# Bringing the inverted triangular blocks back with full transposes instead of small products

## The chip, the cores and the metric

The kernel runs on one of the eight cores of a Trainium2 chip. The metric is device time in microseconds (us) of one execution. A core has five engines with instruction queues of their own that work strictly in order: TensorE (PE; its weight loads are listed as PEld), VectorE (DVE), ScalarE (ACT), GpSimd (POOL) and SyncE (SP, which here only issues transfers).

## The reference, cut to what matters

One layer of a hybrid backbone runs on 640 tokens (128 of a prompt, 512 of a sample). Its second branch is a two-directional recurrence over the tokens, for 8 heads with 64 features:

```python
def step(S, inp):
    r_t, w_t, k_t, v_t, a_t, b_t = inp
    sa = jnp.einsum('bhvk,bhk->bhv', S, a_t)
    S = S * w_t[:, :, None, :] + sa[..., None] * b_t[:, :, None, :] + v_t[..., None] * k_t[:, :, None, :]
    return S, jnp.einsum('bhvk,bhk->bhv', S, r_t)
```

Each step needs `sa`, which depends on the state that the step before left. If 64 tokens are taken as one chunk, all `sa` of a chunk solve a linear system whose matrix is unit triangular, 64 by 64. There are 10 chunks, 8 heads and 2 directions, so 160 such matrices have to be inverted.

## The kernel before, in words

The heads are treated in four pairs, i = 0 to 3. For a pair, `rw_a` projects the inputs and `rw_b` prepares them. `rw_c` writes the within-chunk products of 40 matrices (2 heads, 2 directions, 10 chunks) to `MS`, 128 partitions by 40 by 128; its left upper 64 by 64 holds the triangular part. `rw_i` inverts the two diagonal 32 by 32 blocks of each, `rw_m` joins them to the inverse of the whole and runs the recurrence over the chunks, `rw_e` and `rw_f` give the outputs. `rw_d` transposes keys and values between them (L593, L603) and copies them out (L595, L604).

`rw_i` is the part that changes. It puts one block on each partition: 40 blocks of the first diagonal position (b = 0) on partitions 0 to 39, 40 of the second on 64 to 103. L620 does this with 64 small products by the identity, L622 copies the result to `X` as `X[block, s, t]`. Then come 30 elimination steps on DVE, each a product of two broadcast slices (L629) and an add into `X` (L632). All 60 instructions depend on the one before. Column t of the blocks is final after step t - 1, and from then on L638 brings it back: for each t and each b a product with `X[rows, :, t]` as the stationary operand and the identity as the moving one, 64 in all, each of 40 by 32. Three PSUM banks collect 11, 11 and 10 columns, and L640 copies each bank into `MS`, first DVE for b = 0, then ACT for b = 1.

Nothing fixes the order of the queues by hand. The program is written as a list, a scheduler estimates when each instruction could run, and gives every engine a fixed order. The recurrence is written with high priority. Between its pieces lie the *fills*, 24 blocks of the dense input projection (`values`, `qk_head`, `gate`), which keep PE at work: each is 48 products with 128 stationary columns (L202, L203, L204) on weights which SP loads (L183), ACT rounds (L186) and POOL splits (L187). At the end of a group DVE takes two columns out of PSUM first (L232), then ACT copies the rest.

Of the kernel before, what the change touches and what calls it, by code (L numbers as in the profile page):

```python
# [14 lines left out]
ALU = mybir.AluOpType  # L15
# [20 lines left out]
HJ, HR = 99, 6  # L36
# [30 lines left out]
def tile_layer(ctx, tc, x_prompt, x_sample, cache_k, cache_v, state_rwkv, c, c_ctx, w_ada, b_ada, w_in,  # L67
# [4 lines left out]
    nc = tc.nc  # L72
# [54 lines left out]
    def ada_steps(c0, n, load, ps, small):  # L127
        """n modulation columns from c0, a step for each block of the conditioning vector"""
# [62 lines left out]
    def dense(slabs, kb, xh, xl, evac, extra=0, new=None):  # L191
        """products of a block of weights; the operand's extra leading columns go with the first half"""
# [30 lines left out]
    # the shift of either conditioning in two columns, then the scaled tokens  # L223
# [3 lines left out]
    def project_in(w, evac, scale=1.0, new=None):  # L227
        """a block of the input projection: evac(columns of tokens, products, the shift's part times scale)"""
# [33 lines left out]
    with tc.tile_pool(name="start", bufs=1) as sp, tc.tile_pool(name="psS", bufs=2, space=PSUM) as psS:  # L262
# [21 lines left out]
        def ada1(ps, was, turned, dst, bias):  # L284
            """modulation of 256 features for each of was, the conditioning vector in two halves"""
# [28 lines left out]
        # silu of the conditioning vectors, as the stationary operand  # L314
# [7 lines left out]
        # the scaled input, and with it the first two blocks  # L322
# [27 lines left out]
        # the shift, and its part in the first blocks  # L350
# [21 lines left out]
        # derived per-feature scalars  # L372
# [51 lines left out]
    # the low-rank inputs: what rounds exactly twice over, for the two parts of the weights, and the rest  # L424
# [36 lines left out]
    def rsqrt_heads(x, op, floor):  # L461
        """1/sqrt of the sums of x over each head's features, token-major [token, block, head]"""
# [9 lines left out]
    def spread(rn):  # L472
        """token-major [token, block, head] to feature-major, every feature of a head alike"""
# [12 lines left out]
    def rw_b(i):  # L486
        r, kr, v, upw = (R[i][k] for k in ("r", "kr", "v", "upw"))
        # normalised key
# [65 lines left out]
        # bonus weights  # L554
# [8 lines left out]
    def rw_c(i):  # L563
        AR, BK, v, vrev = (R[i][k] for k in ("AR", "BK", "v", "vrev"))
        # within-chunk products
# [19 lines left out]
    def rw_d(i):  # L585
        BK, v, vrev = (R[i][k] for k in ("BK", "v", "vrev"))
        # token-major values and keys
# [20 lines left out]
    def rw_i(i):  # L608
        MS = R[i]["MS"]
        # inverse of the unit triangular part, in blocks of 32, a block on each partition  # L610
# [3 lines left out]
        prev = None  # L614
        for y in range(2):
# [5 lines left out]
            for b in range(2):  # L621
                (nc.scalar.copy if b else nc.vector.tensor_copy)(out=X[64 * b:64 * b + 40, :, 16 * y:16 * y + 16],  # L622
                                                                 in_=ps[64 * b:64 * b + 40].rearrange("p t s -> p s t"))
# [821 lines left out]
```

## Time and profile before

| | us |
|---|---|
| three runs | 1439.34, 1444.38, 1454.81 |
| median | 1444.38 |
| span of the profiled execution | 1442.3 |
| PE busy | 1334.4 (93%) |
| DVE busy | 928.1 (64%) |
| ACT busy | 535.7 (37%) |
| POOL busy | 556.6 (39%) |

The profiled execution is listed by its span, from the first to the last instruction; a time of its own is not listed beside it. The span lies 2.1 us under the median of the three runs. A page of the profile gives shares over the whole span. The four inversions lie between 127 and 613 us, so the answers that matter are those for stretches in this part, and the order of single instructions in them.

### The profile page before, as it was taken

How to read it: one execution, taken by the hardware profiler on the slowest of the kernel's cores; microseconds unless marked ns; L12 is line 12 of the kernel's file. 1: busy time of each engine (PE TensorE's matmuls, PEld its weight loads, DVE VectorE, ACT ScalarE, POOL GpSimd, SP SyncE). 2: the span in 40 equal slices, each digit the busy share in tenths (PEclk: the TensorE clock that was granted, in tenths of full speed). 3: DMA queues.
4: the chain of work that ended last, by engine and by line, in shares of the span. 5: the costliest groups of instructions: out<-in, count | busy, mean ns of one | idle time of the engine just before them, and what ended most of it. 6: DMA issues, size and time to landing. Idle time of an engine off the chain costs nothing.

```text
span 1442.3 us, 26589 instructions
## 1 busy us (share of the span) xinstructions
PE 1334.4 (93%) x10545; PEld 1139.9 (79%) x10545; DVE 928.1 (64%) x1719; ACT 535.7 (37%) x1126; POOL 556.6 (39%) x423
## 2 busy tenths in 40 slices
PE   6989998899998999999989998968999999999994
PEld 5877877777787778777978777748988989989983
DVE  2476856675568563743136744497897987778777
ACT  3442342234323431242345532254443433434432
POOL 3251225332443132111331036546654735536623
PEclk9997999899799995999999999978999999999997
DMA  9410212211122110111786767513232232322222
GB/s 304 128 56 23 60 38 76 81 55 38 30 82 90 33 47 21 55 51 51 223 268 198 250 205 254 190 45 117 74 103 70 78 95 64 91 67 80 67 68 86
DMA packets 157456, 144.58 MB, mean 100 GB/s; under 512 B 10490, under 2 KB 128020, under 8 KB 157332
## 3 DMA queue, kind: packets, MB, share of 16 engines
q1 hardware_dynamic: 147490, 127.85, 28.9%
q10 hardware_dynamic: 9842, 15.03, 3.1%
q8 instruction: 83, 1.36, 0.4%
q14 instruction: 41, 0.34, 0.1%
HBM read 121.06 MB, written 19.69 MB: 98 GB/s over the span
## 4 chain that ended last, share of the span: by engine, by line
PE 38%; DVE 13%; issue 5%; POOL 3%; DMA 2%; ACT 2%; SPq 1%; DVEq 0%; ACTq 0%; POOLq 0%
PE ps_d L1262 8%; PE ps_e L1262 3%; PE ps_d L202 2%; PE ps_d L203 2%; PE ps_d L204 2%; PE acc L1298 2%; DVE sums L1235 2%; PE acc L1296 2%; PE acc L1297 2%; PE acc L1098 2%; DVE zacc L1311 2%; PE S L964 1%; PE T L988 1%; PE ps_m L749 1%; POOL wl L210 1%
## 5 line engine op out<-in xcount | busy, mean ns | idle before, releaser
L187 POOL TENSOR_TENSOR wl<-ws,wh 128x512 fp32r<-128x512 f32 x100 | 138.6, 1387 | 435.6 <-ACT wh L186 374.8
L210 POOL TENSOR_TENSOR wl<-sums,wh 128x512 fp32r<-128x512 f32 x88 | 136.8, 1560 | 39.2 <-ACT wh L209 37.3
L1262 PE MATMUL ps_d<-oph,wh 128*128 128x320 f32 x440 | 138.5, 315 | 10.6 <-DVE u L1274 5.0
L210 POOL TENSOR_TENSOR wl<-wu,wh 128x512 fp32r<-128x512 f32 x63 | 88.6, 1406 | 142.8 <-ACT wh L209 129.4
L1262 PE MATMUL ps_d<-oph,wl 128*128 128x320 f32 x440 | 137.6, 313 | 0.6 <-POOL wl L210 0.6
L1262 PE MATMUL ps_d<-opl,wh 128*128 128x320 f32 x440 | 137.4, 312 | 0.7 <-DVE opl L210 0.7
L186 ACT CAST wh<-ws 128x512 fp32r<-128x512 f32 x100 | 61.8, 619 | 181.8 <-PE ps_d L203 89.5
L203 PE MATMUL ps_d<-hl,wh 128*128 128x322 f32 (+1 forms) x368 | 128.1, 348 | 0.0
L202 PE MATMUL ps_d<-hh,wh 128*128 128x322 f32 (+1 forms) x368 | 126.6, 344 | 0.7 <-ACT raw L395 0.7
L204 PE MATMUL ps_d<-hh,wl 128*128 128x322 f32 (+1 forms) x368 | 127.0, 345 | 0.0
L1262 PEld LDWEIGHTS ps_d<-oph,wh 128*128 128x128 f32 x440 | 83.7, 190 | 15.0 <-ACT wh L209 7.7
L1262 PEld LDWEIGHTS ps_d<-opl,wh 128*128 128x128 f32 x440 | 83.7, 190 | 2.0 <-POOL hf L1192 1.1
L1262 PEld LDWEIGHTS ps_d<-oph,wl 128*128 128x128 f32 x440 | 83.7, 190 | 1.4 <-POOL wl L210 1.2
L1296 PE MATMUL acc<-wh,gh 128*128 128x512 f32 x195 | 77.5, 398 | 2.5 <-ACT gh L209 2.5
L209 ACT CAST wh<-sums 128x512 fp32r<-128x512 f32 x88 | 54.6, 620 | 65.3 <-PE ps_e L1262 25.3
L202 PEld LDWEIGHTS ps_d<-hh,wh 128*128 128x128 f32 x368 | 74.6, 203 | 5.2 <-issue 1.5
L203 PEld LDWEIGHTS ps_d<-hl,wh 128*128 128x128 f32 x368 | 74.3, 202 | 4.5 <-issue 0.9
L204 PEld LDWEIGHTS ps_d<-hh,wl 128*128 128x128 f32 x368 | 74.0, 201 | 4.3 <-issue 0.8
L1297 PE MATMUL acc<-wl,gh 128*128 128x512 f32 x195 | 77.3, 397 | 0.0
L1298 PE MATMUL acc<-wh,gl 128*128 128x512 f32 x195 | 76.1, 397 | 0.5 <-DVE gl L210 0.5
L203 PE MATMUL ps_x<-hl,wh 128*128 128x322 f32 (+1 forms) x224 | 75.5, 337 | 0.0
L204 PE MATMUL ps_x<-hh,wl 128*128 128x322 f32 (+1 forms) x224 | 74.6, 334 | 0.5 <-POOL wl L187 0.5
(425 smaller groups left out, 3532.2 us busy)
## 6 DMA issues: line engine op xcount, KB each, us to landing
wu<-in_w_up_dram SPq DMA_DIRECT2D x42, 512.0 KB
ws<-in_w_in_dram SPq DMA_DIRECT2D x76, 256.0 KB
wa<-in_w_ada_dram SPq DMA_DIRECT2D x24, 512.0 KB
ws<-in_w_down_dram SPq DMA_DIRECT2D x44, 256.0 KB
wa<-in_w_ada_dram SPq DMA_DIRECT2D x8, 1024.0 KB
ks<-qk_dram SPq DMA_DIRECT2D x32, 192.0 KB
g_dram<-tg ACTq DMA_DIRECT2D x16, 320.0 KB
tg<-g_dram SPq DMA_DIRECT2D x16, 320.0 KB
```

What stands on the lines that cost most here:

```text
L186: nc.scalar.copy(out=wh, in_=ws)
L187: (lo_eng or nc.gpsimd).tensor_tensor(out=wl, in0=ws, in1=wh.bitcast(F32), op=ALU.subtract)
L202: nc.tensor.matmul(pd, wh[:, k, :], xh[:, g, sl], start=g == 0, stop=False)
L203: nc.tensor.matmul(pd, wh[:, k, :], xl[:, g, sl], start=False, stop=False)
L204: nc.tensor.matmul(pd, wl[:, k, :], xh[:, g, sl], start=False, stop=g == kb - 1)
L209: nc.scalar.copy(out=hi, in_=src)
L210: (lo_eng or nc.vector).tensor_tensor(out=lo, in0=src, in1=hi.bitcast(F32), op=ALU.subtract)
L1098: nc.tensor.matmul(ps, lhs, w, start=k == 0 and q == 0, stop=k == KB - 1 and q == 2)
L1262: nc.tensor.matmul(ps, w[:, k, :], x[:, b, k, :], start=k == 0 and z == 0, stop=k == 3 and z == 2)
L1296: nc.tensor.matmul(acc, a_h, wh, start=first, stop=False)
L1297: nc.tensor.matmul(acc, a_h, wl, start=False, stop=False)
L1298: nc.tensor.matmul(acc, a_l, wh, start=False, stop=last)
```

## The change

`X` is kept transposed, as `X[block, t, s]`. The copies from the first products (L622) are then straight, and the elimination (L629, L632) walks the transposed slices: the same element counts per step, with the inner run j instead of 31 - j. The 64 small products of a pair are gone. In their place eight transposes take 128 of the 1024 columns of `X` each, that is four values of t, for all 104 partitions. Each gives 128 by 104: partition 32 q + s holds t = 4 u + q. Two banks take four transposes each. From each bank 8 copies (4 values of q, 2 of b), alternately by DVE and ACT, write to `MS` with a step of four columns, so there are 16 copies of 32 by 160 for a pair, where there were 6 of 32 by 440 or 400. The diff also drops comments throughout, which are left out here.

```diff
@@ rw_i
             for b in range(2):
-                (nc.scalar.copy if b else nc.vector.tensor_copy)(out=X[64 * b:64 * b + 40, :, 16 * y:16 * y + 16],
-                                                                 in_=ps[64 * b:64 * b + 40].rearrange("p t s -> p s t"))
-        nc.vector.memset(X.rearrange("p s t -> p (s t)")[:, ::33], 1.0)
+                (nc.scalar.copy if b else nc.vector.tensor_copy)(out=X[64 * b:64 * b + 40, 16 * y:16 * y + 16, :], in_=ps[64 * b:64 * b + 40])
+        Xf = X.rearrange("p t s -> p (t s)")
+        nc.vector.memset(Xf[:, ::33], 1.0)
         for j in range(1, 31):
-            parts = (((0, j),) if j < HJ else ((0, HR), (HR, j)))
-            tv = tmp[:, 0:j * (31 - j)].rearrange("p (r t) -> p r t", t=31 - j)
-            for r0, r1 in parts:
-                nc.vector.tensor_tensor(out=tv[:, r0:r1], in0=X[:, r0:r1, j:j + 1].broadcast_to([104, r1 - r0, 31 - j]),
-                                        in1=X[:, j:j + 1, j + 1:32].broadcast_to([104, r1 - r0, 31 - j]), op=ALU.mult)
-            for r0, r1 in parts:
-                nc.vector.tensor_tensor(out=X[:, r0:r1, j + 1:32], in0=X[:, r0:r1, j + 1:32], in1=tv[:, r0:r1], op=ALU.add)
-        for t0, n in ((0, 11), (11, 11), (22, 10)):
+            n = 31 - j
+            tv = tmp[:, 0:j * n].rearrange("p (t r) -> p t r", r=j)
+            nc.vector.tensor_tensor(out=tv, in0=X[:, j:j + 1, 0:j].broadcast_to([104, n, j]),
+                                    in1=X[:, j + 1:32, j:j + 1].broadcast_to([104, n, j]), op=ALU.mult)
+            nc.vector.tensor_tensor(out=X[:, j + 1:32, 0:j], in0=X[:, j + 1:32, 0:j], in1=tv, op=ALU.add)
+
+        for y in range(2):
             ps = bank(psR, "m", 2)
-            for t in range(n):
+            for u in range(4):
+                c0 = 128 * (4 * y + u)
+                prev = chain(prev, nc.tensor.transpose(out=ps[:, 104 * u:104 * u + 104], in_=Xf[:, c0:c0 + 128], identity=ident[0:104, 0:104]))
+            for q in range(4):
                 for b in range(2):
-                    rows = slice(64 * b, 64 * b + 40)
-                    prev = chain(prev, nc.tensor.matmul(ps[32 * b:32 * b + 32, 40 * t:40 * t + 40], X[rows, :, t0 + t], ident[rows, rows], start=True, stop=True))
-            for b in range(2):
-                (nc.scalar.copy if b else nc.vector.tensor_copy)(out=MS[32 * b:32 * b + 32, :, 32 * b + t0:32 * b + t0 + n],
-                                                                 in_=ps[32 * b:32 * b + 32, 0:40 * n].rearrange("p (t c) -> p c t", c=40))
+                    t0 = 32 * b + 16 * y + q
+                    (nc.scalar.copy if b else nc.vector.tensor_copy)(
+                        out=MS[32 * b:32 * b + 32, :, t0:t0 + 13:4],
+                        in_=ps[32 * q:32 * q + 32, 0:416].rearrange("p (u r) -> p r u", u=4)[:, 64 * b:64 * b + 40, :])
```

In the changed file the elimination is at L629 and L631, the transposes are at L637 and the copies at L641.

PE in the elimination of pair 0. Before, a pair of small products (L638) stands after every three to six dense products:

```order
L204 MATMUL ps_d<-hh,wl 128x322
L202 MATMUL ps_d<-hh,wh 128x322
L638 MATMUL ps_m<-ident,X 32x40 x2
L203 MATMUL ps_d<-hl,wh 128x322
L204 MATMUL ps_d<-hh,wl 128x322
L202 MATMUL ps_d<-hh,wh 128x320
L203 MATMUL ps_d<-hl,wh 128x320
L204 MATMUL ps_d<-hh,wl 128x320
L638 MATMUL ps_m<-ident,X 32x40 x2
```

Now, later in the same elimination, with a transpose of `X` (L637) and the first key transposes of `rw_d` (L603):

```order
L202 MATMUL ps_x<-hh,wh 128x322
L203 MATMUL ps_x<-hl,wh 128x322
L603 MATMUL ps_m<-ident,BK_892 128x128 x4
L204 MATMUL ps_x<-hh,wl 128x322
L202 MATMUL ps_x<-hh,wh 128x322
L203 MATMUL ps_x<-hl,wh 128x322
L637 MATMUL ps_m<-ident,X 128x104
L204 MATMUL ps_x<-hh,wl 128x322
```

Over the four eliminations the small products stood in 118 places of PE's order; the transposes stand in 32. Counted from the first small product of L620 to the last that brings a block back, PE's order had 157, 132, 158 and 134 dense products in the four pairs (581) and now has 167, 136, 166 and 148 (617); the transposes of L603 in it were 0, 0, 7 and 3, and are 10, 12, 4 and 10.

DVE at the first copies to `MS` in pair 0. Before, it waits for PE alone:

```order
L629 TENSOR_TENSOR tmpx<-X 104x210 [waits DVE_49]
L640 COPY MS<-ps_m 32x40x11 [waits PE_49]
L632 TENSOR_TENSOR X<-X,tmpx 104x10x21 [waits DVE_49]
L629 TENSOR_TENSOR tmpx<-X 104x220 [waits DVE_49]
L632 TENSOR_TENSOR X<-X,tmpx 104x11x20 [waits DVE_49]
```

Now the second and later copies of a bank wait for ACT, in the middle of the elimination:

```order
L641 COPY MS<-ps_m 32x40x4 [waits PE_49]
L631 TENSOR_TENSOR X<-X,tmpx 104x16x15 [waits DVE_49]
L406 SCALAR_TENSOR_TENSOR shtmp<-raw_101,vT,shtmp 128x642 [waits Activation_49]
L629 TENSOR_TENSOR tmpx<-X 104x240 [waits DVE_49]
L641 COPY MS<-ps_m 32x40x4 [waits Activation_49]
L631 TENSOR_TENSOR X<-X,tmpx 104x15x16 [waits DVE_49]
L407 SCALAR_TENSOR_TENSOR v<-raw_101,vT,shtmp 128x128
L629 TENSOR_TENSOR tmpx<-X 104x238 [waits DVE_49]
L641 COPY MS<-ps_m 32x40x4 [waits Activation_49]
```

ACT at the same place. Before, its copy (L640) stood behind one weight cast (L186); now the copies of a bank have a cast between them, which itself waits for a transfer, PE and POOL:

```order
L490 ACTIVATE kk<-kr,vT 128x640
L641 COPY MS<-ps_m 32x40x4 [waits DVE_49]
L186 CAST wh<-ws 128x512 [waits DMAHW7_49,PE_49,Pool_49]
L641 COPY MS<-ps_m 32x40x4 [waits DVE_49] x3
```

DVE and ACT thus hand a bank to and fro: three times per bank DVE's next copy waits for ACT's last one.

## Rows read from the trace of the kernel before

**Rows 1.** Page, part 1: engine, busy us, share of the span, instructions.

```profile
PE 1334.4 (93%) x10545; PEld 1139.9 (79%) x10545; DVE 928.1 (64%) x1719; ACT 535.7 (37%) x1126; POOL 556.6 (39%) x423
```

**Rows 2.** Stretch behind the last inversion: length, busy us per engine, PE's clock, DMA.

```profile
613.00:680.00 67.00, 66.10 (x839) 52.36 (x837) 25.91 (x75) 23.68 (x61) 10.83 (x8) 1.00 0.15 46
```

**Rows 3.** The same view: four eliminations, first product to last add; PE, PEld, DVE, ACT, POOL.

```profile
132.97:171.05 38.08, 37.91 (x292) 30.56 (x291) 32.89 (x78) 12.35 (x24) 8.89 (x7) 0.97 0.18 53
271.73:311.97 40.24, 34.61 (x257) 27.57 (x257) 35.24 (x75) 9.56 (x19) 16.40 (x12) 0.88 0.24 75
418.35:461.79 43.44, 37.59 (x283) 29.83 (x281) 38.82 (x79) 11.87 (x25) 17.21 (x14) 0.97 0.32 101
576.49:611.35 34.86, 33.87 (x264) 26.69 (x263) 25.67 (x70) 8.81 (x19) 6.38 (x5) 0.97 0.19 57
sum 156.62, PE 143.98 PEld 114.65 DVE 132.63 ACT 42.60 POOL 48.89; mean PE 35.99 PEld 28.66 DVE 33.16 ACT 10.65 POOL 12.22
```

**Rows 4.** Timeline, PE around one pair of small products: start us, duration us, instruction.

```profile
157.66 0.31 PE L204 MATMUL ps_d<-hh,wl 128*128 128x320 f32 x1
157.89 0.31 PE L638 MATMUL ps_m<-ident,X 40*32 40x40 f32 x4
158.13 0.41 PE L202 MATMUL ps_d<-hh,wh 128*128 128x320 f32 x1
158.38 0.30 PE L203 MATMUL ps_d<-hl,wh 128*128 128x320 f32 x1
```

**Rows 5.** Timeline, PE around one full transpose between dense products.

```profile
164.12 0.31 PE L204 MATMUL ps_x<-hh,wl 128*128 128x322 f32 x1
164.27 0.31 PE L202 MATMUL ps_x<-hh,wh 128*128 128x320 f32 x1
164.42 0.27 PE L593 MATMUL ps_m<-ident,v 128*128 128x128 f32 x1
164.45 0.39 PE L203 MATMUL ps_x<-hl,wh 128*128 128x320 f32 x1
164.68 0.31 PE L204 MATMUL ps_x<-hh,wl 128*128 128x320 f32 x1
```

**Rows 6.** Timeline, DVE in elimination 3: first step, two waits (in brackets).

```profile
576.49 0.19 DVE L629 TENSOR_TENSOR tmpx<-X 104x30 f32<-104x30 f32 x1
576.71 0.19 DVE L632 TENSOR_TENSOR X<-X,tmpx 104x30 f32<-104x30 f32 x1
...
583.96 0.16 DVE L232 TENSOR_SCALAR bs<-ps_d 128x2 f32<-128x2 f32 x1 [3.29 <-PE ps_d L204]
...
586.69 0.60 DVE L640 COPY MS<-ps_m 32x440 f32<-32x440 f32 x1 [0.72 <-PE ps_m L638]
```

**Rows 7.** Timeline, DVE and POOL in elimination 0: a lengthened add.

```profile
139.55 1.28 POOL L187 TENSOR_TENSOR wl<-ws,wh 128x512 fp32r<-128x512 f32 x1 [6.02 <-ACT wh L186]
139.64 1.40 DVE L632 TENSOR_TENSOR X<-X,tmpx 104x184 f32<-104x184 f32 x1
```

**Rows 8.** Line L640: count, ns min/median/max, first and last start, forms.

```profile
L640 DVE COPY MS<-ps_m x12: 561/604/605, 144.3 to 612.2; 32x440 f32<-32x440 f32 x8, 32x400 f32<-32x400 f32 x4
L640 ACT COPY MS<-ps_m x12: 484/518/562, 145.3 to 613.5; 32x440 f32<-32x440 f32 x8, 32x400 f32<-32x400 f32 x4
```

**Rows 9.** Timeline, the last copies of pair 0 and what follows on DVE.

```profile
171.55 0.56 DVE L640 COPY MS<-ps_m 32x400 f32<-32x400 f32 x1
172.20 0.49 ACT L640 COPY MS<-ps_m 32x400 f32<-32x400 f32 x1
...
173.67 1.50 DVE L646 STREAM_TRANSPOSE Y<-MS 32x1280 f32<-32x1280 f32 x1 [0.85 <-PE ps_m L603]
```

**Rows 10.** Timeline, ACT: a weight cast that waited.

```profile
126.94 0.62 ACT L186 CAST wh<-ws 128x512 fp32r<-128x512 f32 x1 [14.40 <-PE ps_d L203]
```

**Rows 11.** Stretches of four us in eliminations 1 and 2, columns as in Rows 3.

```profile
286.00:290.00 4.00, 2.56 (x22) 2.00 (x22) 3.53 (x10) 0.00 (x0) 0.00 (x0) 0.50 0.47 127
430.00:434.00 4.00, 2.29 (x18) 1.94 (x19) 3.93 (x6) 0.00 (x0) 2.42 (x2) 1.00 0.22 66
```

## The prediction

> **What bounds the kernel now.** I read the page first: PE is busy for 93% of the span, DVE for 64% [rows 1]. That makes PE the engine to free, but it says nothing of the stretch in which the change lies. So I took the stretches next. Behind the last inversion PE works 66.1 of 67.0 us at the full granted clock of 2.4 GHz [rows 2]: what is taken from PE there, or no longer has to be done there, shortens the run. The four eliminations look different [rows 3]. They last 156.6 us together, PE is busy for 144.0 of that and DVE for 132.6. Both are nearly full, so the reader has to see which of them is left when the other gets quicker.
>
> The timeline of PE shows why it is full. Dense products start every 0.15 us [rows 5]. Where a pair of small products stands between them (four instructions, two for each product), 0.72 us pass from one dense product to the next but one, in place of 0.29: the break costs 0.43 us [rows 4]. The products themselves are short. What is paid is the change from a dense product to a small tile and back.
>
> On DVE the 60 steps of an elimination follow each other at a gap of 0.03 us [rows 6]. Each of four eliminations has 60, so 240 gaps take 7.2 us. Of the 24.0 us in which DVE wasn't busy [rows 3] about 16.8 us are left as real waits, and the two longest kinds wait for PE: for the end of a dense group (3.29 us in one place) and for the small products of a bank (0.72 us) [rows 6].
>
> **The change, part by part.**
>
> *The small products go.* They stand in 118 places of PE's order, at 0.43 us each [rows 4]: 50.7 us of PE's time. The lower end is the nearest other row: if such a break costs no more than that of a full transpose, 0.12 us [rows 5], it is 14.2 us. I take the upper, since it is measured in the place itself. Here the Trainium skill speaks against the change (TensorEngine Tiling (Array Packing), Instruction Overhead): a matmul costs about 60 cycles however few columns it has. By that page the 512 instructions would cost 12.8 us at 2.4 GHz (an estimate), and the whole time would come out near the rival below that has this price; the trace disagrees by a factor of four.
>
> *The transposes come.* 32 of them, each in a place of its own. The nearest row is a full transpose of another tile between dense products: from 164.27 to 164.68 two dense steps take 0.41 us in place of 0.29, so it costs 0.12 us [rows 5]. The upper end is the break of a small pair, 0.43 us [rows 4], since a transpose waits for the elimination as the pair did. That is 3.8 to 13.8 us; I take 3.8, because tile shape and neighbours are those of the row. PE then wins 46.9 us, or 36.9 by the other end.
>
> *What of it shortens an elimination.* PE's work there would fall to about 144.0 - 46.9 = 97 us, and DVE's stays at 132.6 busy and 7.2 of gaps [rows 3, 6]. So DVE's chain becomes the bound, and an elimination can give back no more than DVE's waits, 16.8 us in all four. Not all of it comes back. Early in an elimination DVE still waits for the ends of dense groups, and at each first bank DVE still waits for the transpose behind its last add. Some 5 of the 16.8 us stay by my estimate: 0.72 us for each of four banks [rows 6], and 0.5 us in each elimination for the group's end. The gain is 12 us; its ends are 0 and 16.8.
>
> *What is drawn in.* The scheduler fills the freed time: 617 dense products instead of 581 stand in the eliminations, and 36 instead of 10 transposes of L603. 36 at 0.15 and 26 at 0.12 us [rows 5] make 5.4 + 3.1 = 8.5 us of PE's work that is done beside DVE's chain and not in the PE-bound stretches behind it. I take it whole; the other end is 0, where the stretches between are held by the recurrence.
>
> *The elimination itself* is walked in transposed order. A step has the same elements, and a long and a short inner run change places. I cost it at nothing. The first step with 30 elements in one run takes 0.19 us [rows 6]; if short runs cost more, every step pays, on the chain that now bounds: 0.05 us on each of 240 would be 12 us, and that is the upper end. Below nothing I see no reason. The adds that a split of weights on POOL lengthens (1.40 us beside a split of 1.28 [rows 7]) stay: the number of splits is the same. The straight copies into `X` are costed at nothing too; the same count is read from the same bank.
>
> *The copies to `MS`.* 440 and 400 elements took 604 and 561 ns on DVE [rows 8], 1.08 ns for each element, so 160 take about 0.30 us. ACT's 518 and 484 ns give 0.28 us in the same way. DVE and ACT took a bank in turn: ACT starts 0.09 us after DVE's end [rows 9]. In the eliminations DVE had 8 copies of 0.60 us and has 16 of 0.30, which is the same. At the end of an inversion DVE's four copies and ACT's three between them take 4 x 0.30 + 3 x 0.28 + 6 x 0.09 = 2.6 us where one copy of 0.56 us stood, before the transpose of L646, which already waited 0.85 us for something else [rows 9]. So `rw_m` starts 1.2 us or so later for each pair. PE has 20 to 28 dense products queued in that place, so it is mostly covered; I take 0.5 us for each of four pairs, +2 us, and up to 5 uncovered.
>
> *The added wait.* DVE's second, third and fourth copy of a bank wait for ACT's copy before them, 24 times in all, and behind them on DVE stand the next steps of the elimination, for which PE's next transpose waits. On ACT a weight cast often stands in between (0.62 us [rows 10]). I cost it at nothing, because steps of the elimination stand between most copies, 0.65 us each with what lies among them (156.6 us [rows 3] over 240). What it costs without that cover is a rival below.
>
> **The sum** against the profiled execution: -12.0 - 8.5 + 2.0 = -18.5, and 1442.3 becomes 1423.8 us. The median of the runs lies 2.1 us above this span, so I forecast **1426 us**, 1.3% less.
>
> **The rivals.**
>
> *The elimination gives nothing back.* If DVE's waits turn into waits for other things (the transpose of a bank, ACT's copies), only the work that is drawn in counts, and the later `rw_m` is paid: 1442.3 - 8.5 + 5 + 2.1 = 1441 us. For it: PE and DVE are both nearly full [rows 3]. Against it: the longest waits of DVE are for PE [rows 6]. 0.20.
>
> *The clock falls.* PE will wait more often for DVE's chain. Between 286 and 290 us, when PE was busy for 2.56 of 4 us with small pieces, the granted clock was 0.50, that is 1.2 GHz; between 430 and 434 us, with 2.29 us of mostly dense products, it stayed at 1.00 [rows 11]. Four us at half clock do the work of two, so a fall costs 2 us. If it falls twice in each elimination, that is 16 us, of which the waits there hide a part, say 6: 1426 + 10 = 1436 us. The trace does not decide it. 0.13. The Trainium skill has a rule for this (TensorE: Matmul & The Clock Gate, Part 4: PE-mode transpose): transposes do not count as busy for the clock. By it this case is the likelier one; between dense products, as the transposes stand here, no row shows a fall of the clock, so I don't raise its chance.
>
> *The breaks are cheap.* If the rest of the 0.43 us is a wait that would come anyway, a place gives back only the 0.12 us of [rows 5]: 14.2 - 3.8 = 10.4 us, and with the later `rw_m` 1442.3 - 10.4 + 2 + 2.1 = 1436 us. PE was already waiting for nothing in the break shown, which speaks against it [rows 4]. 0.03. The tiling page of the Trainium skill would have it so.
>
> *Slower: the copies tie DVE to ACT's queue.* A cast on ACT waits until PE has left a buffer of weights (14.4 us in one place [rows 10]), DVE's next copy waits behind it, the elimination stands, and PE waits for the next transpose. If a hand-over costs 0.77 us on the average, 24 of them eat the gain of 18.5 us; that is the point from which this case decides. With two casts and a wait, 1.6 us, it is 38 us: 1426 + 38 = 1464 us. Against it: three weight buffers lie between a cast and the products that it waits for. 0.07.
>
> *PE's whole gain counts.* If DVE's chain gets shorter too, for instance because fewer adds meet a split of POOL, up to 40 us come back: 1404 us. Nothing in the rows says so. 0.05.
>
> **How the numbers follow.** The forecast has 0.52. Its lower end is 16.8 and 8.5 us of gain with nothing lost, 1419 us; on the other side 3 us more for the copies and half of the 12 us for short runs give 1435. Two runs of the kernel differ by up to 1%, about 14 us, so about 1% is what a measurement can tell from no change. For 8 in 10 the range runs from 1412 us, where a part of the last rival is in, to 1446 us, which takes in the three cases without a gain to speak of. Faster by over 1% means under 1430 us: most of the forecast and the last rival, 0.54. Within 1%: the first three rivals and the forecast's upper part, 0.39. Slower by over 1%: the copies' case, 0.07.
>
> **What would show it.** Each step has its place in the profile of the changed kernel. The four eliminations should last 140 to 150 us in all, with DVE busy for more than 90% of that and PE's waits named after the adds of L631. A transpose of L637 should delay the dense products by 0.1 to 0.2 us. DVE's waits for ACT before L641 should come to less than 4 us in all. The granted clock in the eliminations should stay at 0.9 or above. The stretch from the last elimination to the attention should be shorter by some 5 us. I am wrong if the eliminations don't get shorter, or if L641 on DVE stands idle behind casts of ACT.

## The result and the profile after

| | before | change |
|---|---|---|
| median of 20 runs each, us | 1444.39 | 1434.26 |
| span of the profiled execution, us | 1442.3 | 1430.8 |
| mean granted clock, median over runs (before: 76 runs, change: 20) | 0.940 | 0.940 |

The ratio is 0.9932 with a 95% interval of [0.9915, 0.9949]: the change makes the kernel 0.7% faster, 10 us, where 1.3% and 18 us were forecast. The median lies inside the range, but that says little, since the range (1412 to 1446 us) takes in no change at all as well; and the class with the highest chance, faster by over 1% (0.54), did not come. The mechanism is the one forecast: in the eliminations PE gets work off and DVE's chain becomes the bound. Its gain there was larger than forecast. What failed is a later step, the work that is "drawn in": the stretches between the inversions lost work by it and still got longer, by waits of PE.

Page of the changed kernel, part 1, answering to [rows 1]:

```profile
PE 1293.1 (90%) x10065; PEld 1115.5 (78%) x10065; DVE 926.1 (65%) x1739; ACT 543.8 (38%) x1146; POOL 567.6 (40%) x423
```

PE is busy for 41.3 us less, yet the span is only 11.5 us shorter: PE's time without work rose from 107.9 to 137.7 us. That difference is the question of this study.

The four eliminations of the change, columns as in [rows 3]:

```profile
133.49:169.49 36.00, 30.54 (x195) 27.52 (x194) 33.11 (x82) 14.03 (x29) 8.51 (x7) 0.98 0.22 63
279.08:314.46 35.38, 27.23 (x161) 24.48 (x159) 33.08 (x78) 11.43 (x25) 13.09 (x9) 0.92 0.23 69
437.92:474.12 36.20, 29.20 (x178) 26.55 (x176) 34.35 (x78) 12.16 (x27) 15.40 (x11) 0.94 0.33 104
572.43:603.64 31.21, 26.37 (x168) 24.31 (x166) 28.74 (x73) 11.05 (x24) 8.16 (x6) 0.96 0.23 74
sum 138.79, PE 113.34 PEld 102.85 DVE 129.27 ACT 48.66 POOL 45.16; mean PE 28.34 PEld 25.71 DVE 32.32 ACT 12.17 POOL 11.29
```

They last 138.8 us instead of 156.6. PE has 113.3 us of work in them, 30.6 less. Before, PE was busy for 92% of them and DVE for 85%; now it is 82% and 93%.

The span splits as follows, worked out from the starts and ends of these instructions in both traces: 17.8 us are gained in the eliminations, 4.3 are lost from the last add to the transpose that opens `rw_m` (L646 before, L648 now; 14.0 us in all before, 18.3 now), 6.3 in the stretches from there to the next elimination (310.9 and 317.2), 4.8 are gained behind the last inversion (827.8 and 823.0), and 0.5 are lost ahead of the first. The stretches from L648 to the next elimination, first before, then now:

```profile
sum 310.88, PE 298.14 PEld 241.50 DVE 171.23 ACT 106.13 POOL 102.79; mean PE 99.38 PEld 80.50 DVE 57.08 ACT 35.38 POOL 34.26
```

```profile
174.69:279.08 104.39, 95.59 (x1093) 77.89 (x1092) 56.49 (x115) 33.65 (x80) 42.52 (x33) 0.91 0.21 63
318.97:437.92 118.95, 109.39 (x1091) 87.44 (x1091) 63.76 (x130) 38.39 (x87) 44.58 (x33) 0.79 0.15 44
478.62:572.43 93.81, 88.53 (x1075) 70.76 (x1074) 53.41 (x120) 33.43 (x78) 25.26 (x19) 0.98 0.11 34
sum 317.15, PE 293.50 PEld 236.09 DVE 173.66 ACT 105.47 POOL 112.36; mean PE 97.83 PEld 78.70 DVE 57.89 ACT 35.16 POOL 37.45
```

PE has 4.6 us less to do there and waits 10.9 us more (23.7 in place of 12.7). The granted clock doesn't explain it: its mean over these stretches is 0.88 before and 0.89 now. Nor does a single odd execution: runs 1 and 8 below keep the queue orders of before and of the change, and their stretches between come to 310 and 318 us.

The dense products show where work moved. 550 start in the eliminations before and 582 now, 35 and 65 on the way from the last add to L648, 594 and 573 in the stretches between, 857 and 816 behind. PE waits for 1.8 us of the 18.3 on the way, so most of what is lost there is work of PE that was done elsewhere before.

PE's waits by the view of waits, from the first elimination's end to the last one's start, in the changed kernel:

```profile
PE ps_m L637 <- DVE X L631: 13.6, 10, 2.9
PE ps_ch L708 <- ACT UV L702: 5.8, 3, 4.4
PE ps_m L481 <- ACT rx L476: 4.9, 4, 1.9
PE ps_m L572 <- DVE MS L577: 4.4, 7, 2.9
PE ps_x L204 <- POOL wl L187: 3.0, 2, 2.7
```

The first line lies in the eliminations and costs nothing there, since DVE sets their length. The second, fourth and fifth are new in this size: before, L572 waited 0.4 us for L577, L204 0.5 for L187, and L706, as the products of L708 were then numbered, had no row. But before, one wait of 4.7 us of L688 for L717 stood in the same stage and is gone, so the second line adds about 1 us net. It still shows how such a wait arises. DVE, ACT and PE of the changed kernel, in the stage where pair 0's recurrence runs beside the preparation of pair 1:

```profile
229.12 1.34 DVE L547 SCALAR_TENSOR_TENSOR BK<-BK,ld 128x640 f32<-128x640 f32 x1
230.38 2.06 DVE L552 TENSOR_TENSOR BK<-ta,ld 128x640 f32<-128x640 f32 x1
233.87 1.65 DVE L557 SCALAR_TENSOR_TENSOR ta<-ta,vT,r 128x640 f32<-128x640 f32 x1 [1.42 <-POOL ta L556]
235.54 0.28 DVE L702 COPY UV<-ps_ch 64x128 f32<-64x128 f32 x1
```

```profile
235.86 0.26 ACT L702 COPY UV<-ps_ch 64x128 f32<-64x128 f32 x1 [6.94 <-DVE UV L702]
236.18 0.70 PE L708 MATMUL ps_ch<-UV,BT 128*64 128x64 f32 x8 [4.37 <-ACT UV L702]
```

```profile
228.00:232.00 4.00, 3.81 (x26) 3.36 (x25) 4.00 (x3) 0.89 (x2) 3.84 (x4) 1.00 0.19 55
232.00:236.00 4.00, 0.00 (x0) 0.00 (x0) 2.54 (x4) 0.14 (x1) 3.92 (x3) 0.72 0.00 0
236.00:240.00 4.00, 3.75 (x20) 2.92 (x20) 3.15 (x4) 1.84 (x5) 3.84 (x4) 0.50 0.06 18
240.00:244.00 4.00, 4.00 (x23) 3.34 (x23) 1.01 (x4) 0.90 (x4) 2.31 (x2) 0.50 0.88 278
```

In DVE's fixed order, the copy of 0.28 us that the recurrence needs (L702) stands behind three long operations of pair 1's preparation, one of which waits for POOL. ACT's half of the same copy waits 6.94 us for DVE's, and PE waits for ACT's, with its dense products queued after L708. Behind the wait the granted clock is 0.50 from 236 to 244 us, so a part of the wait is paid a second time.

### The profile page after: what moved, and what is told of

It reads as the page before. It is cut to its first block, busy times and chain, and to the rows that moved or that the text cites. A ratio compares the mean times of both kernels' runs of the same rounds, so it can differ in the third digit from the quotient of the medians.

```text
span 1430.8 us, 25679 instructions
## 1 busy us (share of the span) xinstructions
PE 1293.1 (90%) x10065; PEld 1115.5 (78%) x10065; DVE 926.1 (65%) x1739; ACT 543.8 (38%) x1146; POOL 567.6 (40%) x423
## 4 chain that ended last, share of the span: by engine, by line
PE 43%; DVE 20%; issue 6%; POOL 4%; ACT 3%; DMA 3%; POOLq 0%; SPq 0%; ACTq 0%; DVEq 0%
PE ps_d L1264 8%; PE ps_e L1264 3%; PE ps_d L202 2%; PE ps_d L203 2%; PE acc L1100 2%; PE ps_d L204 2%; PE acc L1300 2%; DVE tmpx L629 2%; PE acc L1298 2%; DVE X L631 2%; PE acc L1299 2%; POOL wl L210 2%; DVE sums L1237 2%; DVE zacc L1313 1%; PE ps_m L572 1%
## 5 line engine op out<-in xcount | busy, mean ns | idle before, releaser
L187 POOL TENSOR_TENSOR wl<-ws,wh 128x512 fp32r<-128x512 f32 x100 | 139.8, 1398 | 434.2 <-ACT wh L186 353.3
L202 PE MATMUL ps_d<-hh,wh 128*128 128x320 f32 (+1 forms) x368 | 126.9, 345 | 2.6 <-ACT raw L395 1.3
L203 PE MATMUL ps_d<-hl,wh 128*128 128x320 f32 (+1 forms) x368 | 126.6, 344 | 0.0
L204 PE MATMUL ps_d<-hh,wl 128*128 128x320 f32 (+1 forms) x368 | 126.2, 343 | 0.0
L186 ACT CAST wh<-ws 128x512 fp32r<-128x512 f32 x100 | 61.9, 620 | 160.0 <-PE ps_d L203 82.4
L202 PEld LDWEIGHTS ps_d<-hh,wh 128*128 128x128 f32 x368 | 76.5, 208 | 7.0 <-ACT raw L395 2.1
L204 PEld LDWEIGHTS ps_d<-hh,wl 128*128 128x128 f32 x368 | 76.3, 207 | 3.1 <-issue 1.5
L204 PE MATMUL ps_x<-hh,wl 128*128 128x322 f32 (+1 forms) x224 | 73.9, 332 | 3.0 <-POOL wl L187 3.0
L202 PE MATMUL ps_x<-hh,wh 128*128 128x322 f32 (+1 forms) x224 | 74.8, 334 | 1.1 <-ACT wh L186 1.1
```

The costliest lines, as they stand in the source:

```text
L186: nc.scalar.copy(out=wh, in_=ws)
L187: (lo_eng or nc.gpsimd).tensor_tensor(out=wl, in0=ws, in1=wh.bitcast(F32), op=ALU.subtract)
L202: nc.tensor.matmul(pd, wh[:, k, :], xh[:, g, sl], start=g == 0, stop=False)
L203: nc.tensor.matmul(pd, wh[:, k, :], xl[:, g, sl], start=False, stop=False)
L204: nc.tensor.matmul(pd, wl[:, k, :], xh[:, g, sl], start=False, stop=g == kb - 1)
```

## The experiments

Columns: the median; the ratio to the kernel before, measured on the same chip; and from each profiled execution the sums over four pairs of the eliminations, of the way from the last add to the transpose opening `rw_m`, of the three stretches from there to the next elimination, the time behind the last inversion, and PE's time without work (span less PE's busy time). The last column is the median over its runs of the mean granted clock. In the fourth kernel the transpose doesn't wait for the elimination, so the split does not apply. The parts are those of one execution, which need not lie near the median: it took 1427 us in 4, 1437 in 5, 1430 in 6 and 1435 in 7.

| kernel | median us | ratio [95%] | elim. | way | between | behind | PE without work | clock |
|---|---|---|---|---|---|---|---|---|
| before | 1444.4 | | 157 | 14 | 311 | 828 | 108 | 0.940 |
| change | 1434.3 | 0.9932 [0.9915, 0.9949] | 139 | 18 | 317 | 823 | 138 | 0.940 |
| 1 layout alone | 1444.5 | 0.9988 [0.9954, 1.0022] | 159 | 14 | 310 | 825 | 108 | 0.935 |
| 2 products in a block | 1465.4 | 1.0131 [1.0071, 1.0190] | 128 | 52 | 331 | 821 | 141 | 0.913 |
| 3 one hand-over | 1428.4 | 0.9894 [0.9848, 0.9941] | 146 | 11 | 317 | 819 | 128 | 0.935 |
| 4 not brought back | 1433.6 | 0.9932 [0.9896, 0.9968] | | | | | 128 | 0.925 |
| 5 other bank sizes | 1449.5 | 1.0034 [1.0002, 1.0066] | 161 | 10 | 306 | 823 | 106 | 0.933 |
| 6 banks of 4, 3, 1 | 1422.0 | 0.9860 [0.9814, 0.9906] | 128 | 33 | 313 | 819 | 134 | 0.946 |
| 7 ACT has a bank | 1428.7 | 0.9904 [0.9871, 0.9937] | 148 | 10 | 322 | 817 | 130 | 0.935 |
| 8 neighbouring columns | 1431.6 | 0.9923 [0.9894, 0.9953] | 138 | 16 | 318 | 821 | 131 | 0.941 |
| 9 as 6, one hand-over each | 1421.5 | 0.9848 [0.9814, 0.9882] | 131 | 33 | 307 | 816 | 135 | 0.947 |
| 10 recurrence first | 1431.4 | 0.9916 [0.9885, 0.9948] | 153 | 20 | 297 | 825 | 133 | 0.935 |
| 11 as 9 and 10 | 1431.7 | 0.9944 [0.9915, 0.9972] | 137 | 35 | 306 | 817 | 129 | 0.930 |

The clock differs from kernel to kernel, and time goes with it. A straight line through the 76 runs of the kernel before gives 10 us less for each 0.01 of mean clock; the lines of the others give 6 to 13. Read at 0.940 on its own line, the span would be 1441 us before and 1433 for the change, and for runs 1 to 11: 1438, 1437, 1422, 1415, 1441, 1428, 1423, 1429, 1425, 1426 and 1418. These are estimates, and in 2, 4 and 11 they reach well beyond the clocks that their runs had (0.908 to 0.929, 0.921 to 0.932, 0.923 to 0.933). What sets a kernel's mean clock was not tested: a new order may do it, by its waits.

**1. The layout alone.**

```diff
-prev = chain(prev, nc.tensor.matmul(ps[32 * b:32 * b + 32, 40 * t:40 * t + 40], X[rows, :, t0 + t], ident[rows, rows], start=True, stop=True))
+prev = chain(prev, nc.tensor.matmul(ps[32 * b:32 * b + 32, 40 * t:40 * t + 40], X[rows, t0 + t, :], ident[rows, rows], start=True, stop=True))
```

The first copies and the elimination are those of the change.

> The elimination in the transposed layout with its straight copies, but with the 256 small products of the kernel before. Theory A (the gain comes from PE's breaks, the layout is neutral): the four eliminations last 157 us in all, as before, within 3 us, and the time is that of before, 1444 us, within 5. Rival B (the layout itself makes the steps of DVE cheaper): the eliminations last about 139 us as in the change, and the time is about 1434 us.

The queues keep the order of the kernel before, and the time is the same within 0.5%. The layout is not the cause, and the fear that short inner runs cost every step is gone too. (The eliminations came to 159 us, 157 in the kernel before: that of pair 0 had a mean clock of 0.79 in place of 0.97 and took 5 us more.)

**2. The small products in one block.**

```diff
-        for t0, n in ((0, 11), (11, 11), (22, 10)):
+        for t0, n in ((21, 11), (10, 11), (0, 10)):
-            for t in range(n):
+            for t in reversed(range(n)):
```

> The kernel before, but its 64 small products of a pair in reversed order, so that all stand in one block behind the last add. Theory A (what costs is the 118 changes between dense products and small tiles, not the products): PE's work in the eliminations falls by about 33 us as in the change, and they last 132 to 138 us in all; behind the last add 64 products and the copies come to about 6.5 us in place of 3.5, which is 12 us more in all, so the time lies near 1436 us. Rival B (full transposes are cheaper than small products as such, wherever they stand): PE keeps its work, nothing is won, and the later end of the inversion makes it 1450 us or more.

The eliminations fell to 128 us, further than expected. PE without the breaks, sum of the four:

```profile
sum 127.80, PE 97.60 PEld 94.54 DVE 118.83 ACT 32.76 POOL 48.01; mean PE 24.40 PEld 23.63 DVE 29.71 ACT 8.19 POOL 12.00
```

And the block behind the last add of pair 0:

```profile
166.88 3.15 PE L638 MATMUL ps_m<-ident,X 40*32 40x40 f32 x88 [2.12 <-DVE X L632]
169.96 0.69 PE L807 MATMUL ps_d<-ident,vt 128*128 128x128 f32 x2
170.58 1.55 PE L638 MATMUL ps_m<-ident,X 40*32 40x40 f32 x40
```

The clock in it, columns as in [rows 3]:

```profile
168.00:170.00 2.00, 2.00 (x63) 1.91 (x58) 0.60 (x1) 0.52 (x1) 0.00 (x0) 0.50 0.37 110
```

128 instructions take 4.7 us, 37 ns each, and that at a granted clock of 0.50; between dense products four of them cost 0.43 us [rows 4]. (That row is typical: over the 86 places of the eliminations before that have one such pair between dense products at the full clock, the median from one dense product to the next but one is 0.73 us.) So it is the place between dense products that costs, not the product: rival B is out. The wait for the elimination, which the block has only once, is not the reason either, since the transposes of the change wait for it one by one and cost 0.19 us in the place shown further below. That leaves the change of tile. The Trainium skill's overhead of some 60 cycles for each matmul (TensorEngine Tiling (Array Packing), Instruction Overhead) would be 50 ns at the 1.2 GHz of this block, an estimate; the block's 37 ns lie below it, and the rule says nothing of the changes of tile.

The time was wrong for A all the same: 1465 us. The way to L646 came to 52 us in place of the expected 26, for `rw_d`'s transposes and dense products came to stand ahead of it, with PE busy all the while at a granted clock of 0.66 to 0.73. The kernel also has the lowest mean clock of all, 0.913; read at 0.940 it would be near the 1436 us that A expected, so the clock can account for the miss.

**3. One hand-over for a bank.**

```diff
-            for q in range(4):
-                for b in range(2):
+            for b in range(2):
+                for q in range(4):
```

> The change, but from each bank DVE copies its four parts first, then ACT its four: one hand-over for a bank in place of seven. Theory A (the hand-overs cost about 8 us behind the last adds, which the recurrence waits for, and nothing within the eliminations): from the last add to L648 about 2.5 us in place of 4.6 for each pair, and a time of 1426 us (the change 1434). Rival C (what the copies cost is hidden beside PE's dense products): the stretch from the last add is shorter, the time stays at 1434 us.

DVE at the end of pair 0's inversion, first in the change, then here:

```profile
169.30 0.19 DVE L631 TENSOR_TENSOR X<-X,tmpx 104x30 f32<-104x30 f32 x1
169.89 0.43 DVE L641 COPY MS<-ps_m 32x160 f32<-32x160 f32 x1 [0.40 <-PE ps_m L637]
170.18 0.67 DVE L604 COPY BT<-ps_m 128x512 f32<-128x512 f32 x1
171.41 0.43 DVE L641 COPY MS<-ps_m 32x160 f32<-32x160 f32 x1 [0.57 <-ACT MS L641]
172.43 0.44 DVE L641 COPY MS<-ps_m 32x160 f32<-32x160 f32 x1 [0.59 <-ACT MS L641]
172.90 0.69 DVE L810 COPY vs<-ps_d 128x512 f32<-128x512 f32 x1
173.62 0.43 DVE L641 COPY MS<-ps_m 32x160 f32<-32x160 f32 x1
174.09 0.69 DVE L604 COPY BT<-ps_m 128x512 f32<-128x512 f32 x1
174.69 1.49 DVE L648 STREAM_TRANSPOSE Y<-MS 32x1280 f32<-32x1280 f32 x1
```

```profile
171.13 0.19 DVE L631 TENSOR_TENSOR X<-X,tmpx 104x30 f32<-104x30 f32 x1
171.72 1.77 DVE L641 COPY MS<-ps_m 32x160 f32<-32x160 f32 x4 [0.40 <-PE ps_m L637]
173.53 0.69 DVE L604 COPY BT<-ps_m 128x512 f32<-128x512 f32 x1
174.13 1.49 DVE L648 STREAM_TRANSPOSE Y<-MS 32x1280 f32<-32x1280 f32 x1
```

From the last add to L648 it is 5.2 us (169.49 to 174.69) and then 2.8 (171.32 to 174.13); over four pairs 18 and 11. The time fell by 6 us against the change (1434.3 to 1428.4, each against its own runs of the kernel before), 2 us above what A expected, and its interval overlaps the change's: that the hand-overs are paid, as A says, is likely but not shown. The eliminations grew by 7 us with the new order, so the gain didn't come from them.

**4. Not brought back at all.**

```diff
-        for y in range(2):
-            ps = bank(psR, "m", 2)
...
-                        in_=ps[32 * q:32 * q + 32, 0:416].rearrange("p (u r) -> p r u", u=4)[:, 64 * b:64 * b + 40, :])
```

> The change without the eight transposes and the copies: the inverted blocks are not brought back at all, which bounds what any way of bringing them back can give. Theory A (DVE's chain is what an elimination now lasts): DVE is without 16 copies of 0.43 us, about 122 us of work remain, the eliminations last 128 us in all, L648 follows at once, and the time falls to 1410 to 1420 us. Rival D (what PE saves returns as waits behind the inversions): the eliminations shorten as said, but the stretches between them grow, and the time stays above 1428 us.

1433.6 us: a kernel with no bring-back at all, whose recurrence doesn't even wait for the elimination, is no faster than the change. The time is D's and not A's, but neither's mechanism can be read from it: with nothing waiting for them the eliminations lasted 159 us in all, not 128, and the kernel has the second lowest clock, 0.925. Read at 0.940 it would lie at 1415 us, within A's range; so whether the saving came back as waits or only as lost clock is open. Nor is it the bound that was meant, since 9 brings the blocks back and is 12 us faster. PE, part 1 of its page (span 1425.0):

```profile
PE 1297.4 (91%) x10033; PEld 1125.4 (79%) x10033; DVE 908.9 (64%) x1707; ACT 530.1 (37%) x1114; POOL 559.9 (39%) x423
```

**5. A change of order with nothing to gain.**

```diff
-        for t0, n in ((0, 11), (11, 11), (22, 10)):
+        for t0, n in ((0, 10), (10, 11), (21, 11)):
```

> The kernel before, with the 32 columns in banks of 10, 11 and 11 instead of 11, 11 and 10: the same instructions on every engine but for two copies of other size, yet the scheduler gives the queues another order. Theory A (the stretches between the inversions take what the order and the granted clock make of them, whatever the inversion gives): the eliminations stay at 155 to 160 us, the stretches between them move by 5 to 15 us either way, and the time lies between 1434 and 1458 us, not at 1444. Rival E (the order is all but neutral, and the losses seen between the inversions come from the change itself): 1444 us within 3.

The eliminations came to 161 us, the stretches between went from 311 to 306 and the ways from 14 to 10. The median lies 5.5 us above before on the same chip (1443.99), within A's range and outside E's, though the interval only just leaves out no change, and at the same clock nothing is left of it (1441 us in both). So a new order alone moves the parts by some 5 us, which is nearly the size of the 6.3 that the change lost between the inversions. It does not raise PE's time without work: 106 us.

**6, 7 and 9. Fewer copies on DVE.** In 6, three banks, the first two by ACT alone; in 9 only the first by ACT. 7 has the change's two banks, the first by ACT and the second with one hand-over.

The banks of 6 and 9:

```diff
-        for y in range(2):
+        for u0, n in ((0, 4), (4, 3), (7, 1)):
```

The condition of a copy, in 6, 9 and 7:

```diff
-                    (nc.scalar.copy if b else nc.vector.tensor_copy)(
+                    (nc.scalar.copy if b or u0 < 7 else nc.vector.tensor_copy)(
```

```diff
+                    (nc.scalar.copy if b or u0 == 0 else nc.vector.tensor_copy)(
```

```diff
+                    (nc.scalar.copy if b or not y else nc.vector.tensor_copy)(
```

> The change with three banks of 4, 3 and 1 transposes; ACT copies the first two banks alone, and the last one, which waits for the last add, is a single transpose with 8 copies of 32 by 40, four on DVE and then four on ACT. Theory A (DVE's chain bounds an elimination, and the way from the last add to L648 is paid): DVE has no copies in the eliminations, so they last about 132 us in all in place of 139, L648 comes about 2 us after the last add in place of 4.6, and the time is 1419 us plus or minus 10 for the order. Rival D (what an inversion gives back returns as waits and half clock behind it): both get shorter as said, and the time stays at 1428 to 1434 us.

> The change with the first bank copied by ACT alone and the second by DVE (four) and then ACT (four). Theory A: eliminations about 132 us in all, L648 2.8 us after the last add as in the kernel with one hand-over, time 1422 us plus or minus 10 for the order. Rival D: the inversions are shorter as said, the time stays at 1428 to 1434 us.

> Three banks of 4, 3 and 1 transposes as in the run before, but ACT has only the first bank alone; the second and third are copied by DVE (four) and then ACT (four). Theory A: ACT's late copies made L648 come 8.3 us after the last add; now it comes in about 2.5 us, and DVE has 4 x 0.37 us more in an elimination. Eliminations about 133 us in all, the ways to L648 10 us, 143 us together (the change 157, the run before 161), and a time of 1415 us plus or minus 10 for order and clock. Rival D (it returns as waits behind the inversions): 143 us as said, but the time stays at 1422 us or above.

6 and 9 are the fastest, 1422.0 and 1421.5 us, 1.4 and 1.5% under before. In both, the eliminations are as short as A said (128 and 131 us), but L648 comes some 8 us after the last add, not 2.5: `rw_d`'s transposes and their copies (L595, L604) have moved behind the last add, and L648 stands behind them in DVE's queue. So the way to L648 is not simply paid, as A had it: PE waits only 3 to 5 of these 33 us, and works off what it would otherwise do elsewhere. Both times lie within A's ranges, and 6 lies below D's; the 1421.5 us of 9 don't tell it from D's 1422. In 7 the way is 10 us as expected, the eliminations are 148 us, not 132, and the time is 1428.7: undecided between A and D. Part of the lead of 6 and 9 is their clock of 0.946 and 0.947. Read at 0.940, their spans would be 1428 and 1425 us, those of 3 and 7 1422 and 1423: at the same clock nothing of the lead is left over these two.

**8. Neighbouring columns.**

```diff
-                    t0 = 32 * b + 16 * y + q
+                    t0 = 32 * b + 16 * y + 4 * q
-                        out=MS[32 * b:32 * b + 32, :, t0:t0 + 13:4],
+                        out=MS[32 * b:32 * b + 32, :, t0:t0 + 4],
```

> The change with each copy written to four neighbouring columns of MS in place of four columns at a step of four, which puts the columns of the inverse in a wrong order. The order of every queue is that of the change. If the step of 16 bytes makes the copies long, a copy takes 0.30 us in place of 0.43, about 16 of the 64 copies stand one behind the other between a last add and L648 of the four pairs, and 2 us in all come back: 1432 us. If the number of short runs in PSUM makes them long, a copy stays at 0.43 us and the time at 1434 us.

Line L641, the change first (count, ns min/median/max, first and last start):

```profile
L641 DVE COPY MS<-ps_m x32: 412/432/458, 149.9 to 607.3; 32x160 f32<-32x160 f32 x32
L641 ACT COPY MS<-ps_m x32: 415/433/447, 150.4 to 607.8; 32x160 f32<-32x160 f32 x32
```

```profile
L641 DVE COPY MS<-ps_m x32: 302/317/326, 151.0 to 606.2; 32x160 f32<-32x160 f32 x32
L641 ACT COPY MS<-ps_m x32: 281/284/288, 151.3 to 606.6; 32x160 f32<-32x160 f32 x32
```

The prediction's 0.30 and 0.28 us hold for neighbouring columns; the step of four costs 0.12 us on DVE and 0.15 on ACT. The time of 1431.6 is what was expected, but the two intervals overlap. The same order gave the same waits as the change (L702 4.6 us, L577 4.4, L187 2.9), which shows that they belong to the order and not to one execution.

**10 and 11. The recurrence ahead of the preparation.**

```diff
-    rw_m(0)
+    hp(lambda: rw_m(0))
```

> The change, with rw_m of pair 0 written at the same priority as the preparation of pair 1, so that DVE has the copies of the recurrence (L702) ahead of the long operations of rw_b (L547, L552, L557) and not behind them. Theory A (the waits that are new between the inversions come from the order of DVE's queue): the wait of 4.4 us of L708 for L702 near 236 us is gone, with it the stretch at half clock behind it, the stretch from L648 of pair 0 to the elimination of pair 1 is shorter than the 104.4 us of the change by 4 to 8 us, and the time is 1426 to 1430 us unless the later rw_b makes PE wait in its place. Rival F (the recurrence is then ahead, but PE lacks rw_b's results at the end of the stretch): the stretch stays at 104 us or longer, with a wait for L557 or L577 in its place, and 1434 us or more.

> The kernel with banks of 4, 3 and 1 transposes (DVE and ACT hand over once in the last two), and rw_m of pair 0 at the priority of pair 1's preparation. Theory A (the two gains add): the wait of 3.8 us of L708 for L702 near 244 us is gone and the kernel is 3 us quicker than without the priority, 1415 to 1420 us. Rival G (the long operations of rw_b only move into the elimination of pair 1, as with the change itself, where the eliminations grew from 139 to 153 us): the stretch behind pair 0 is 10 us or more shorter, the eliminations that much longer, and the time stays at 1422 us or above.

In 10 the wait of L708 is gone. The first stretch between and the four eliminations:

```profile
175.90:267.90 92.00, 89.81 (x1036) 71.24 (x1035) 51.36 (x110) 30.94 (x74) 35.40 (x28) 0.88 0.18 52
...
sum 153.10, PE 114.39 PEld 103.11 DVE 140.43 ACT 50.02 POOL 54.57; mean PE 28.60 PEld 25.78 DVE 35.11 ACT 12.51 POOL 13.64
```

The stretch is 12.4 us shorter, more than A expected, and PE's waits in the three stretches fall from 23.7 to 9.8 us. But the eliminations are 14 us longer: DVE has 140.4 us of work in them where it had 129.3, since the work that no longer stands ahead of L702 lies there now, on the engine that bounds them. The time is 3 us less than the change's, and the intervals overlap. F's wait didn't come; the loss came in a third way, DVE's work, which G had named.

In 11 the wait of L708 is gone too, but the time is 1431.7 us. The eliminations grew by 6 us; the stretch behind pair 0 shrank by 6 (107.6 to 101.7), not the ten that G named, and the three together by 1. The mean clock is 0.930 where 9 has 0.947, which at 10 us for 0.01 is more than the whole difference, so whether the gains add at the same clock is open.

## Why the prediction was right, and where it was wrong

*The small products.* Right. The 30.6 us that PE lost in the eliminations, with 32 more dense products (4.7 us), 33 more transposes of `rw_d` (4.0) and 28 of L637 at 0.19 us (5.3), make about 45 us for the 111 places that lay within the eliminations, 0.40 us each by this estimate in place of 0.43. Run 2 and the cost of L637 leave the change of tile as the reason.

*The transposes.* They cost more than the 0.12 us taken, and lie in the range given:

```profile
135.72 0.31 PE L202 MATMUL ps_d<-hh,wh 128*128 128x320 f32 x1
135.91 0.28 PE L637 MATMUL ps_m<-ident,X 104*128 104x104 f32 x1
135.97 0.39 PE L203 MATMUL ps_d<-hl,wh 128*128 128x320 f32 x1
136.20 0.31 PE L204 MATMUL ps_d<-hh,wl 128*128 128x320 f32 x1
```

0.48 us pass from L202 to the next dense product but one, in place of 0.29, so this one costs 0.19. Over the eight places in the eliminations where one stands so, without a wait and at the full clock, the median is 0.53 us.

*What of it shortens an elimination.* Right in mechanism, too small in size: 17.8 us, not 12. DVE's time without work fell from 24.0 to 9.5 us, of which 7.2 are gaps. I had left 5 us of real waits; about 2 stayed. Within the eliminations the waits for the small products (L640, 5.6 us) and for the transposes of `rw_d` (L595, 2.6) are gone, and those at a dense group's end (L232) fell from 8.6 to 1.0 us. The other 3.3 us are DVE's busy time, which I had taken as fixed: 1.9 of it are the steps themselves, of which 25 in place of 28 took over 1 us, and the rest is other work. So the gain passed the 16.8 us that I had called its end, and the 138.8 us of the eliminations lie just under the 140 to 150 that I had named as a sign.

*The copies.* The term was 2 us. The way to L648 got 4.3 us longer, because the step of four columns lengthens a copy (run 8) and DVE waits for ACT 6.6 us in all, where I had said less than 4. Only 1.2 us of these waits lie within the eliminations: the elimination steps that I had named as cover hold there, and not behind the last add. The other cover, PE's queued dense products, did hold: PE waits 1.8 us on these ways, and 30 more dense products start on them.

*What is drawn in.* **This is the step that failed.** The work did move: 32 more dense products start within the eliminations and 30 more on the ways to L648, 41 fewer behind L648 of the last pair, and 4.8 us came back there. But I took the whole 8.5 us as gain and looked for no loss in the stretches between. These gave off the other 21 dense products, and got 6.3 us longer all the same. Their order was made anew, and with it came 10.9 us more of waits of PE, the new ones mostly for DVE and POOL. So the part between and behind gave +1.5 us where -8.5 was forecast; with -17.8, +4.3 and +0.5 the sum is -11.5. That the time came within 8 us of the forecast is in part luck: the 5.8 us that the eliminations gave beyond their term make up for more than half of the 10 that failed here.

*The rivals.* By their times alone two of them, 1436 us each, come nearer to the 1434.3 than the forecast; the traces rule them out. The breaks were not cheap (0.73 us as the median of 86 places, above). That the elimination gives nothing back is out by its 17.8 us. The clock did not fall by the transposes: the eliminations show 0.98, 0.92, 0.94 and 0.96, before 0.97, 0.88, 0.97 and 0.97 [rows 3]. It falls between the inversions, in both kernels, and over the runs both have 0.940, so it does not explain the result. ACT's queue did not tie up the eliminations. PE's whole gain did not count: PE's 41.3 us became 11.5.

*What stays open.* The nine kernels, the change among them, that bring the blocks back without the spread small products all have 128 to 141 us of PE without work, against 106 to 108 us in the three with them. Runs 8 and 10 show that single waits come from the order, and that one moved away can come back as DVE's work elsewhere. Whether some order could turn more of PE's freed time into time is not shown; none was written by hand. How much of the differences between the kernels is the clock is known only from straight lines through few runs, and why a kernel has its mean clock is not known.

## What to carry to other kernels

A small tile between dense products costs the change of tile, not its columns (here 0.43 us for four instructions): look at the pitch of the dense products around it. When such a break goes, the next engine's chain is the bound, and its waits in that stretch are about what comes back there (16.8 us of waits here, 17.8 gained). Work "drawn in" to a stretch is a gain only if the stretch it leaves was bound by that work: look at what stands ahead of the small copies on the in-order engines before counting it. And read the clock beside each time: here its spread between kernels, 0.913 to 0.947, is worth as much as their differences in time, by the estimate of 10 us for 0.01.

## What the runs showed that was not expected

A copy of 32 by 160 written at a step of four columns takes 0.43 us in place of 0.32 on DVE and 0.28 on ACT (run 8). A stage of small products alone ran at either level of the clock, the same level from end to end. The output products of pair 1 (L749 before, L751 now) took 15.3 us before, from 379.4 to 394.7, and 9.8 in the change, from 396.9 to 406.7, with hardly a dense product among them. Before, the stretch that holds the fall (PE waits in it) and the one behind it:

```profile
376.00:380.00 4.00, 3.23 (x15) 2.19 (x15) 3.64 (x5) 2.92 (x8) 2.04 (x1) 0.67 0.01 4
380.00:384.00 4.00, 4.00 (x44) 2.92 (x43) 4.00 (x8) 1.28 (x4) 2.22 (x2) 0.50 0.20 49
```

In the change, where 17 dense products start between 392 and 396 us, just ahead of the stage, and the granted clock rises from 0.50 to 1.00 in those four us:

```profile
396.00:400.00 4.00, 4.00 (x55) 2.83 (x55) 4.00 (x5) 2.44 (x6) 1.49 (x2) 1.00 0.07 16
400.00:404.00 4.00, 4.00 (x66) 2.95 (x62) 3.44 (x7) 0.22 (x1) 3.40 (x3) 1.00 0.36 98
```
